# Pads that move the weight pool and the general slots to multiples of 2048 bytes

## The chip, the cores and the metric

One core of one Trainium2 chip runs the whole program. The metric is the device time in microseconds from launch to end; the kernel before is timed at 1852.68 us, the median of 3 runs (1852.58 to 1853.74).

## What is computed

Two layers of a bidirectional encoder on 512 tokens of width 1024, all in fp32. Each layer is half a feed-forward block, a mixer, and half a feed-forward block again:

```
for layer in range(2):
    x = x + 0.5 * swiglu(rms_norm(x), w_gate, w_up, w_down)      # width 2816
    x = x + mixer(rms_norm(x))     # layer 0: dilated attention | Fourier; layer 1: latent attention | S5
    x = x + 0.5 * swiglu(rms_norm(x), w_gate, w_up, w_down)
```

## The kernel before

Tokens lie along the free dimension: an activation tile is 128 channels (partitions) by 512 tokens of 4 bytes, 2048 bytes in each partition. A product that must be good to fp32 is made of three matmuls of type fp32r: each operand is split into a high and a low part, and `mm3` (L136 to L145) multiplies high with high, high with low, low with high. Each of the three is cut into two halves of 256 tokens, and each matmul loads its stationary operand anew:

```
cs = (slice(0, n // 2), slice(n // 2, n)) if n == 512 else (slice(0, n),)
for i, (l, r) in enumerate(((0, 0), (0, 1), (1, 0))):
    for j, c in enumerate(cs):
        mm(out[:, c], lhs[l], rhs[r][:, c], ...)
```

In the trace a matmul is two records: LDWEIGHTS (engine PEld, 128 columns of the stationary operand, 512 bytes of each partition) and MATMUL (engine PE, 256 columns of the moving operand, 1024 bytes of each partition). The trace has 14,592 MATMULs of this line, L145, most of them in the four feed-forward blocks.

On-chip memory (bytes within a partition) is cut into pools, one behind the other, in the order in which `Trunk.__init__` makes them: `const` (gains, x, tables, `ident`), `wp` (the weights: three raw buffers, two high `w_hi`, two low `w_lo`, 8192 bytes each), `tiny` (statistics), `sp` (60 general slots of 2048 bytes: split activations `xgh`, `xgl`, `ah`, `al`, and everything else 512 tokens wide). In front of `const` lies a reserved scratch of 16,384 bytes.

The three pairings of stationary and moving operand that matter here:

- Feed-forward gate and up (outputs `pg`, `pu`) and down (`pd<-ah`, `pd<-al`): the stationary operand is 128 columns of a weight buffer, the moving one half of a slot.
- The input projections of the mixers (`pz`, `pkvu`): the stationary operand is a slot, the moving one a weight buffer.
- Some products of the mixers: both operands lie in slots. Such are the first column block of the output projection (`pd<-mgh,owh` and the like, whose weights `owh`, `owl` are kept in slots), the scores of layer 1 (`sc<-kTh,qTh`), `pq` and `pglu`.

Weights are streamed: `Weights.next` (from L75) has the raw buffers loaded by SyncE up to two units ahead, ScalarE copies a unit to `w_hi` (L49), VectorE makes `w_lo` (L50), while TensorE works on the unit before. A scheduler lays down each engine's instruction order when the program is built. A feed-forward block is two halves, each of 11 gate/up units (96 matmuls each) and 8 down units (66 matmuls each). Between units stand a few matmuls of other shapes: the column sums of the norm (`msc`, L381), the transposes of its result (`rows`, L233), and in two blocks of the S5 tables (`s_pg`, `s_pk`).

Of the kernel before, what the change touches and what calls it, by code (L numbers as in the profile page):

```python
# [5 lines left out]
F32 = mybir.dt.float32  # L6
# [10 lines left out]
HF = NF // 2  # L17
HT = S // 2 + 2
EPS = 1e-6


def f32(ap):
# [3 lines left out]
class Weights:  # L26


    def __init__(self, nc, pool):
        self.nc, self.pool, self.eng = nc, pool, None  # L30
        self.units, self.raw, self.ready = [], {}, {}
        self.pos = self.loaded = self.cut = 0
# [59 lines left out]
class Trunk:  # L92
    def __init__(self, ctx, tc, t):
        self.tc, self.nc, self.t = tc, tc.nc, t
        nc = self.nc
        self.const = ctx.enter_context(tc.tile_pool(name="const", bufs=1))
        self.wp = ctx.enter_context(tc.tile_pool(name="wp", bufs=2))
        self.tiny = ctx.enter_context(tc.tile_pool(name="tiny", bufs=3))
        self.sp = ctx.enter_context(tc.tile_pool(name="sp", bufs=60))
        self.ps = ctx.enter_context(tc.tile_pool(name="ps", bufs=8, space=PSUM))  # L100
        self.W = Weights(nc, self.wp)
        self.gains = self.const.tile([128, 6 * KD], F32, name="gains")
        nc.sync.dma_start(self.gains, t["gains"])
        self.ones = self.const.tile([128, 128], F32, name="ones")
        nc.vector.memset(self.ones, 1.0)
        self.x = [self.const.tile([128, S], F32, name=f"x{c}", tag=f"x{c}") for c in range(KD)]
        self.ident = self.const.tile([128, 128], F32, name="ident")

    def start(self, norm):

        nc = self.nc
        load = lambda c: nc.sync.dma_start(self.x[c], self.t["xT"][c])
        w = self.W.first(KD // 2)
        load(0)
        next(w)
        for c in range(2, KD, 2):
            load(c - 1)
            load(c)
            next(w)
        load(KD - 1)  # L120

        p = self.bank("warm")
        for i in range(10):
            nc.tensor.matmul(p[:, 0:128], self.ones, self.ones, start=True, stop=True)
        self.prep_start()
        for c in range(KD):
            self.scale_split(c, norm)
            if c % 2 == 0:
                next(w)
        nc.sync.dma_start(self.ident, self.t["ident"])  # L130
# [245 lines left out]
    def ms_cols(self, eng=None):  # L376
# [5 lines left out]
        v = self.small(4)("msv")  # L382
        nc.vector.tensor_scalar(out=v, in0=p, scalar1=1.0 / D, scalar2=EPS, op0=ALU.mult, op1=ALU.add)
        return v, self.rsqrt(v, self.small(4), eng)
# [24 lines left out]
    def even_mixer(self, after):  # L409
# [7 lines left out]
        for which in range(2):  # L417
            pz = [self.bank("pz") for _ in range(4)]
            for u in range(2):
# [6 lines left out]
                if epx is None:  # L426
                    msx, rsx = self.ms_cols(nc.gpsimd)
                    epx = self.small(4)("epx")
                    nc.vector.tensor_scalar(out=epx, in0=msx, scalar1=EPS, scalar2=None, op0=ALU.mult)
            for q, z in enumerate(self.head_norm(pz, epx, self.q_rope if which == 0 else self.k_rope, which == 1)):  # L430
# [260 lines left out]
    def odd_mixer(self, after):  # L691
# [21 lines left out]
        epx = new4("epx")  # L713
        nc.vector.tensor_scalar(out=epx, in0=msx, scalar1=EPS, scalar2=None, op0=ALU.mult)
        for k in range(KD):
# [20 lines left out]
        for j in range(2):  # L736
            down(pql[j], wh, wl, 256, j * 128, 128)
            ql.append(self.split(pql[j], "ql", self.lat_gain[:, j:j + 1]))
            if j == 0:
# [10 lines left out]
                nc.vector.tensor_reduce(out=kss, in_=kps, axis=AX.X, op=ALU.add)  # L750
                nc.vector.tensor_scalar(out=kss, in0=kss, scalar1=1.0 / 96, scalar2=EPS, op0=ALU.mult, op1=ALU.add)
                self.rotate(kp[:, :, 0:32], 16, self.kc_rope[0], self.kc_rope[1])
# [49 lines left out]
        def query_eps():  # L802
            nc.vector.tensor_scalar(out=eaq, in0=self.lat_ms(qlsq, 256, epx), scalar1=EPS, scalar2=None, op0=ALU.mult)

# [932 lines left out]
```

## Time and profile before

| | |
|---|---|
| median of 3 runs | 1852.68 us |
| the profiled execution's own time | 1853.05 us |
| its span, first to last instruction | 1851.3 us |
| TensorE busy | 1830.1 us, 99% |
| VectorE, ScalarE, GpSimd busy | 53%, 34%, 5% |
| granted TensorE clock over the span | 0.997 |
| bytes moved | 185.65 MB |

A MATMUL's record is longer than its share of the time, because matmuls are pipelined and the records overlap. What a matmul costs in a dense stretch is the distance from one start to the next, here called its pitch: the length of the stretch over the count of matmuls in it.

### The profile page before, as it was taken

To read this page: it belongs to the slowest core of one execution; us is meant where nothing else is said; L and a number is where in the kernel's file an instruction comes from. 1 tells how busy PE (TensorE), PEld (TensorE's weight loads), DVE (VectorE), ACT (ScalarE), POOL (GpSimd) and SP (SyncE) were. 2 spreads that over 40 slices of the span, in tenths; PEclk is the share of its full clock that TensorE was granted. 3 is DMA by queue.
4 is the path that set the end of the run, shared out by engine and by line. 5 is a ranking of instruction groups with operands and counts; after the bars stand their busy time and mean duration, and the time that the engine had idled before them with its cause. 6 is when DMAs were issued, how large, how long until landed. Compare 5 with 4: busy or idle time off the path is not lost.

```text
span 1851.3 us, 35303 instructions
## 1 busy us (share of the span) xinstructions
PE 1830.1 (99%) x15608; PEld 1810.8 (98%) x15608; DVE 986.0 (53%) x1732; ACT 622.6 (34%) x818; POOL 85.4 (5%) x138
## 2 busy tenths in 40 slices
PE   9999999999999999999999999999989999999999
PEld 9999999999799999999999999999988899999999
DVE  5643444456955954556744434444688654434442
ACT  4321222324953222222332222223366632212321
POOL 0000000011120000000000000000045100000000
PEclk9999999999999999999999999999999999999999
DMA  6223221331122325342322233223144222133221
GB/s 209 93 73 121 95 105 64 117 108 68 37 92 92 113 100 150 112 111 100 128 103 92 79 116 110 89 73 109 69 129 141 79 96 103 64 118 113 85 89 67
DMA packets 63447, 185.65 MB, mean 100 GB/s; under 512 B 27424, under 2 KB 28352, under 8 KB 51136
## 3 DMA queue, kind: packets, MB, share of 16 engines
q1 hardware_dynamic: 63296, 183.41, 29.3%
q8 instruction: 122, 2.00, 0.4%
q14 instruction: 29, 0.24, 0.0%
HBM read 170.79 MB, written 10.49 MB: 98 GB/s over the span
## 4 chain that ended last, share of the span: by engine, by line
PE 95%; DVE 2%; ACT 1%; DMA 1%; issue 0%; POOL 0%; SPq 0%; ACTq 0%; POOLq 0%; DVEq 0%
PE pd L145 30%; PE pu L145 27%; PE pg L145 26%; PE pz L145 4%; PE etp L1447 1%; PE sc L145 1%; PE pf L145 1%; PE pql L145 1%; PE s_py L1230 1%; PE pq L145 1%; PE po L1467 0%; PE po L1468 0%; DVE et_lo L1459 0%; PE sc L533 0%; ACT e L1440 0%
## 5 line engine op out<-in xcount | busy, mean ns | idle before, releaser
L49 ACT ACTIVATE w_hi<-w_raw 128x2048 fp32r<-128x2048 f32 (+4 forms) x175 | 288.6, 1649 | 878.3 <-PE pu L145 449.7
L50 DVE TENSOR_TENSOR w_lo<-w_raw,w_hi 128x2048 fp32r<-128x2048 f32 (+4 forms) x172 | 338.2, 1966 | 166.2 <-ACT w_hi L49 166.0
L145 PE MATMUL pu<-xgh,w_hi 128*128 128x256 f32 x1440 | 282.9, 278 | 0.0
L145 PE MATMUL pu<-xgh,w_lo 128*128 128x256 f32 x1440 | 282.8, 278 | 0.0
L145 PE MATMUL pu<-xgl,w_hi 128*128 128x256 f32 x1440 | 282.6, 278 | 0.0
L145 PE MATMUL pg<-xgh,w_hi 128*128 128x256 f32 x1408 | 277.9, 279 | 1.2 <-ACT w_hi L49 1.2
L145 PE MATMUL pd<-al,w_hi 128*128 128x256 f32 x1408 | 277.5, 277 | 0.0
L145 PE MATMUL pd<-ah,w_lo 128*128 128x256 f32 x1408 | 277.4, 277 | 0.0
L145 PE MATMUL pd<-ah,w_hi 128*128 128x256 f32 x1408 | 276.7, 277 | 0.0
L145 PE MATMUL pg<-xgh,w_lo 128*128 128x256 f32 x1408 | 276.5, 278 | 0.0
L145 PE MATMUL pg<-xgl,w_hi 128*128 128x256 f32 x1408 | 276.4, 278 | 0.0
L145 PEld LDWEIGHTS pu<-xgh,w_hi 128*128 128x128 f32 x1440 | 218.7, 189 | 0.0
L145 PEld LDWEIGHTS pu<-xgh,w_lo 128*128 128x128 f32 x1440 | 218.2, 188 | 0.2 <-DVE w_lo L50 0.2
L145 PEld LDWEIGHTS pu<-xgl,w_hi 128*128 128x128 f32 x1440 | 218.2, 188 | 0.0
L145 PEld LDWEIGHTS pg<-xgh,w_hi 128*128 128x128 f32 x1408 | 213.8, 189 | 1.5 <-ACT w_hi L49 1.5
L145 PEld LDWEIGHTS pd<-ah,w_lo 128*128 128x128 f32 x1408 | 213.9, 188 | 0.0
L145 PEld LDWEIGHTS pd<-ah,w_hi 128*128 128x128 f32 x1408 | 213.6, 188 | 0.0
L145 PEld LDWEIGHTS pg<-xgl,w_hi 128*128 128x128 f32 x1408 | 213.4, 188 | 0.0
L145 PEld LDWEIGHTS pg<-xgh,w_lo 128*128 128x128 f32 x1408 | 213.4, 188 | 0.0
L145 PEld LDWEIGHTS pd<-al,w_hi 128*128 128x128 f32 x1408 | 213.4, 188 | 0.0
L255 DVE TENSOR_TENSOR gn<-pg,rows 128x512 f32<-128x512 f32 x88 | 60.7, 689 | 279.3 <-PE pg L145 279.3
L298 DVE SCALAR_TENSOR_TENSOR x<-pd,x 128x512 f32<-128x512 f32 (+1 forms) x65 | 44.4, 684 | 232.5 <-PE pd L145 232.5
(365 smaller groups left out, 2088.6 us busy)
## 6 DMA issues: line engine op xcount, KB each, us to landing
w_raw<-wa SPq DMA_DIRECT2D x86, 1024.0 KB, 4.9
w_raw<-wb SPq DMA_DIRECT2D x64, 704.0 KB, 4.0
w_raw<-we_qkv SPq DMA_DIRECT2D x6, 1024.0 KB, 4.9
w_raw<-we_out SPq DMA_DIRECT2D x3, 768.0 KB, 4.2
w_raw<-wo_out SPq DMA_DIRECT2D x3, 768.0 KB, 4.1
x<-xT SPq DMA_DIRECT2D x8, 256.0 KB, 5.5
dr_h<-s_h SPq DMA_DIRECT2D x8, 256.0 KB, 2.8
dr_g<-s_g SPq DMA_DIRECT2D x8, 256.0 KB, 3.0
```

The costliest lines, as they stand in the source:

```text
L49: self.nc.scalar.activation(hi, raw, AF.Copy)
L50: (self.eng or self.nc.vector).tensor_tensor(out=lo, in0=raw, in1=f32(hi), op=ALU.subtract)
L145: mm(out[:, c], lhs[l], rhs[r][:, c], start=first and i == 0 and j == 0, stop=last and i == 2, skip_group_check=len(cs) > 1)
L255: nc.vector.tensor_tensor(out=gn, in0=pg, in1=rstd, op=ALU.mult)
L298: nc.vector.scalar_tensor_tensor(out=x, in0=p, scalar=0.5, in1=x, op0=ALU.mult, op1=ALU.add)
L1230: nc.tensor.matmul(py[half][:, k, :], m[i][:, i4, :], r[:, k, :], start=i == 0, stop=i == 2)
L1447: nc.tensor.transpose(p[:, kc, :], e[:, kc * 128:kc * 128 + 128], T.ident)
```

## The change

Two tiles that nothing reads are added, one at the end of what `const` holds when `__init__` returns, one at the start of `tiny`; GpSimd writes zeros into each once. The reserved scratch is halved, which gives the room.

```diff
+PAD_CONST, PAD_TINY = 448, 464
...
         self.ident = self.const.tile([128, 128], F32, name="ident")
+
+        for pool, n in ((self.const, PAD_CONST), (self.tiny, PAD_TINY)):
+            nc.gpsimd.memset(pool.tile([128, n], F32, name="pad", bufs=1), 0.0)
...
-    nc = _bacc.Bacc("TRN2", target_bir_lowering=False, num_devices=1)
+    nc = _bacc.Bacc("TRN2", target_bir_lowering=False, num_devices=1, dynamic_dma_scratch_size=8192)
```

Where the built programs put things, in bytes within a partition:

| | before | rest by 2048 | after | rest by 2048 |
|---|---|---|---|---|
| first raw weight buffer | 39168 | 256 | 32768 | 0 |
| first `w_hi`, first `w_lo` | 63744, 80128 | 256 | 57344, 73728 | 0 |
| first slot (all others follow in steps of 2048) | 104896 | 448 | 100352 | 0 |
| `x0` | 17216 | 832 | 9024 | 832 |
| `ident` | 33600 | 832 | 25408 | 832 |

A stationary operand of a feed-forward matmul starts at a multiple of 512 bytes from its buffer's start, a moving one at 0 or 1024 bytes from its slot's. So the two starts differ by 192 bytes, taken by multiples of 512, in every feed-forward matmul before, and by 0 after. Where both operands lie in slots they differ by 0 before and after.

The order of instructions and what each waits for is the same on all engines, line numbers apart, but for GpSimd. Its program begins so before:

```order
L1730 MEMSET const-float32-0.0 128x1
L1730 MEMSET const-float32-1.0 128x1
L1730 MEMSET const-bfloat16-1.0 128x1
L1730 MEMSET const-uint8-127 128x1
L1721 UNCONDITIONAL_BRANCH
L207 ISA
L207 TENSOR_SCALAR rs_i<-msv 128x4
```

and so after:

```order
L1734 MEMSET const-uint8-127 128x1
L1725 UNCONDITIONAL_BRANCH
L111 MEMSET pad 128x448
L111 MEMSET pad 128x464
L211 ISA
L211 TENSOR_SCALAR rs_i<-msv 128x4
```

Two memsets stand between the start and the engine's first work, the reciprocal root of layer 0's mixer norm (`rs_i<-msv`); nothing else moved.

## Rows read from the trace of the kernel before

**Rows 1.** The page: engines' busy time, and the chain by engine.

```profile
PE 1830.1 (99%) x15608; PEld 1810.8 (98%) x15608; DVE 986.0 (53%) x1732; ACT 622.6 (34%) x818; POOL 85.4 (5%) x138
...
PE 95%; DVE 2%; ACT 1%; DMA 1%; issue 0%; POOL 0%; SPq 0%; ACTq 0%; POOLq 0%; DVEq 0%
```

**Rows 2.** The chain in order of time: start us, length us, engine, output, line, matmuls.

```profile
133.25 59.84 PE pd L145 x528
...
372.61 10.88 PE pz L145 x96
...
526.51 26.87 PE pd L145 x228
...
872.74 62.19 PE pd L145 x528
```

**Rows 3.** Timeline of PE, both operands in slots: start us, us, instruction.

```profile
517.82 0.40 PE L145 MATMUL pd<-mgl,owh 128*128 128x256 f32 x2
518.05 0.40 PE L145 MATMUL pd<-mgh,owl 128*128 128x256 f32 x2
...
519.74 0.64 PE L145 MATMUL pd<-mgh,owh 128*128 128x256 f32 x4
```

**Rows 4.** Timeline of PE round the `rows` transposes at 576.7 us.

```profile
576.26 0.40 PE L145 MATMUL pu<-xgl,w_hi 128*128 128x256 f32 x2
576.50 0.40 PE L145 MATMUL pu<-xgh,w_lo 128*128 128x256 f32 x2
576.73 0.60 PE L233 MATMUL rows<-ident,rs_y 128*128 128x128 f32 x4
...
578.57 0.39 PE L145 MATMUL pg<-xgh,w_hi 128*128 128x256 f32 x2
578.80 0.39 PE L145 MATMUL pg<-xgl,w_hi 128*128 128x256 f32 x2
```

**Rows 5.** L145 by stretches: length, PE busy (MATMULs), clock, DMA share, GB/s.

```profile
111.50:383.50 272.00, 271.99 (x2400) 1.00 0.29 101
577.50:643.50 66.00, 65.16 (x575) 1.00 0.31 108
959.00:1302.00 343.00, 342.75 (x3023) 1.00 0.27 94
1510.70:1847.00 336.30, 336.30 (x2969) 1.00 0.26 91
31.50:111.50 80.00, 79.61 (x674) 1.00 0.25 86
384.30:430.00 45.70, 45.05 (x382) 1.00 0.20 70
526.50:577.50 51.00, 50.16 (x423) 1.00 0.29 104
643.50:959.00 315.50, 308.14 (x2595) 1.00 0.36 115
1458.50:1510.70 52.20, 51.36 (x433) 1.00 0.29 102
```

**Rows 6.** Timeline of PE: matmuls with a moving operand of 64 columns.

```profile
1428.42 0.61 PE L1230 MATMUL s_py<-s_x,s_h 128*128 128x64 f32 x4
1428.87 0.39 PE L1230 MATMUL s_py<-s_U,s_t 128*128 128x64 f32 x2
1429.09 0.61 PE L1230 MATMUL s_py<-s_x,s_h 128*128 128x64 f32 x4
```

**Rows 7.** Timeline of POOL: the last instruction at the start, and the next one.

```profile
0.32 0.10 POOL L1730 MEMSET const-uint8-127<- 128x1 uint8 x1
384.56 0.20 POOL L207 TENSOR_SCALAR rs_i<-msv 128x4 int32<-128x4 int32 x1 [384.14 <-DVE msv L383]
```

**Rows 8.** A group of POOL by line: count, busy us, mean ns, idle us before.

```profile
L1152 POOL TENSOR_TENSOR s_sw<-s_sw,s_sin 128x512 f32<-128x512 f32 x8 | 11.1, 1393 | 5.8 <-DMA s_sw<-s_a 5.5 <-issue 0.3
```

**Rows 9.** Waits: who waited for whom, us in total, times, longest us.

```profile
ACT w_hi L49 <- PE pu L145: 449.7, 80, 10.3
```

## The prediction
> **What bounds the kernel now.** I read the page first [rows 1]: TensorE is busy for 99% of the span and makes up 95% of the chain that ends last. VectorE and ScalarE have nearly half their time free or more, and ScalarE waits for TensorE to free a weight buffer, 449.7 us in all behind `pu` alone [rows 9]. So the time is the number of matmuls times their pitch, and only something that changes the pitch, or stops TensorE, can move it.
>
> The second view is the chain in order of time, which gives the pitch of clean stretches [rows 2]. The down product of the first half of a feed-forward block is 528 matmuls of 256 columns without a break. At 133.25 us it takes 59.84 us, 113.3 ns a matmul. At 872.74 us the same code on the same kind of tiles takes 62.19 us, 117.8 ns. The granted clock is 1.00, 2.4 GHz, in both [rows 5]. 256 columns at that clock are 106.7 ns, so 7 to 11 ns a matmul are lost on something that has two states.
>
> The third view is the timeline at places where the state changes [rows 4]. Before the four `rows` transposes at 576.73 us two matmuls start 0.24 us after the two before them; a microsecond behind the transposes they are 0.23 apart, and stay so. The change comes at an interruption of the row of equal matmuls, and the state then lasts for tens or hundreds of us. Hence a table of L145 by stretches, cut at these changes [rows 5]: the first four stretches are in the quick state, 2400 + 575 + 3023 + 2969 = 8967 matmuls; the last five in the slow one, 674 + 382 + 423 + 2595 + 433 = 4507. (Length over count comes out above the pitch where other matmuls, such as those of the tables, stand in a stretch; the pitch is taken from clean rows, [rows 2, 4].) Of the 14,592 matmuls of L145 some 1118 remain: 194 of the first 31 us and about 924 in the mixers.
>
> The fourth view is what this change turns on. In the output projection at 517 us both operands lie in slots [rows 3]: from the start at 517.82 to the one at 519.74 us there are eight rows of two, 16 matmuls, in 1.92 us, **120.0 ns** each. Same shape, same type, same line, same clock, steady; only the addresses are of another kind. There the stationary and the moving operand start at the same place by multiples of 512 bytes; in the feed-forward blocks they start 192 bytes apart. (With the roles exchanged, `pz`: slot stationary, weights moving, also 192 apart, the pitch is 10.88 us / 96 = 113.3 ns [rows 2].) So the trace has three pitches, 113.3 and 117.8 where the starts differ by 192 and 120.0 where they differ by 0.
>
> **The change, part by part.** *Addresses of weights and slots.* Nothing is removed or reordered; the change gives every pair of weight and slot the difference 0, which today only slot with slot has. The nearest row for the new pairs is therefore [rows 3], and I take its 120.0 ns for all of them. That it is the difference that counts, and not where each operand stands by itself, is a choice: in [rows 3] both operands stand at 448 by 2048 (or a multiple of 512 further), after the change both stand at 0. The trace has no matmul of 256 columns with both at 0. I choose the difference because exchanging the roles of the two operands leaves the pitch alone.
> - Quick state: 8967 x (120.0 - 113.3) ns. With unrounded pitches, 59.84 / 528 = 113.33, that is 8967 x 6.67 = +59.8 us.
> - Slow state: 4507 x (120.0 - 117.78) = +10.0 us.
> - In the mixers about 408 matmuls more pair weights with a slot (924, less those with both in slots and a few of 258 columns): at 2.2 ns +0.9 us. Those with both operands in slots stay at 120.0.
> - Sum +70.7 us.
>
> All of it lies on the path, since in these stretches TensorE waits for nothing. No other engine can come to be the bound: all have the same work and more time for it.
>
> *The bounds of this term.* From above: 120.0 is the longest steady pitch that the trace has at this clock for this shape, so +70.7. From below: with a moving operand of 64 columns, which is far too short to be the limit, a matmul starts every 111.7 ns: six from 1428.42 to 1429.09 us [rows 6]. I read this as what loading 128 columns of a stationary operand costs. If the two reads never met, the pitch would fall to it: 8967 x (111.7 - 113.33) + 4915 x (111.7 - 117.78) = -14.6 - 29.9 = -44.5 us (4915 being 4507 and the 408).
>
> *The two memsets.* They stand behind the start on GpSimd, whose next work begins at 384.56 us after a wait of 384.14 us for VectorE [rows 7]. Each costs between 0.10 us, the memset of one column [rows 7], and 1.39 us, the two-operand product of 512 columns [rows 8]. So at most 2.8 us of 384 idle ones: nothing. Nothing is queued behind them that TensorE needs earlier; without that cover they would cost those 2.8 us once.
>
> *The smaller scratch.* All transfers of the kernel are issued by SyncE, none by GpSimd, and the sizes of transfers stay. ScalarE's copies wait for TensorE [rows 9], so the data are there first. I take zero; a loss would have to appear as ScalarE waiting for DMA.
>
> *A rule against it.* The rows say that addresses matter: 120.0 against 113.3 ns [rows 2, 3]. The Trainium skill, "SBUF — State Buffer", section "Who interferes with whom", gives TensorE two independent read ports, one for the moving operand and one for the weight load, and says that TensorE and ScalarE never wait on anyone; by that the pitch could not depend on where the operands lie, and the sum would be 0 instead of +70.7. The trace does not bear that out. [...]
>
> **The sum against the measured time.** The profiled execution took 1853.05 us, 0.37 above the median; outside its span lie 1.75. 1853.05 + 70.7 = 1923.8 for that execution, 1923.4 against the median.
>
> **The rivals.**
> 1. *Both on a boundary: faster.* What costs may be an operand that does not start on a boundary of the memory: one such operand in the feed-forward pairs (448, with 256 for the other), two in [rows 3]. Then 113.3 and 120.0 are one and two penalties, and after the change there is none. The roles can be exchanged here too, so `pz` does not speak against it. Against it: it has no place for the two states of one pair of addresses. It gives the lower bound, 1852.7 - 44.5 = 1808. It decides from the first feed-forward block on: a pitch under 113 ns there.
> 2. *The change does not do what it is meant to: the addresses do not matter.* Then 120.0 comes from what else goes on in the mixers, and the states come from interruptions alone, which stand where they stood: 1852.7. Against it: 120.0 is as steady as the other two, and the products of weights and slots that follow at 526.51 us in the same output projection go back to 26.87 us / 228 = 117.9 ns [rows 2].
> 3. *Only the states fall otherwise.* The pitches stay, but an interruption leaves the other state behind. All quick: 4915 x -4.45 = -21.9, 1831. All slow: 8967 x 4.45 = +39.9, 1893.
>
> **How the numbers follow.** Forecast 0.55 (its own range 1905 to 1935: a pitch of 118.4 to 121); rival 1 0.20; rival 2 0.14; rival 3 0.11, evenly on both sides. Faster: 0.20 + 0.05 = 0.25. Same, within 0.2%, 3.7 us, which is about what a measurement of this kernel can tell from no change: 0.15. Slower: 0.55 + 0.05 = 0.60. The range leaves out rival 1 and reaches from all quick, 1830, to 1935. The prediction is 1923.
>
> **What would show it.** The clean down stretches of 528 matmuls should take 63.4 us in all eight halves (113.3 ns would be 59.8, rival 1 under 59.5), and the two states should be gone: one pitch, not two. Start distances of 0.24 us everywhere. The slot pairs stay at 120.0. GpSimd's memsets should be over by 3 us. If the eight stretches come out in two kinds again, the difference by 512 is not the cause, and the step "the nearest row is rows 3" is wrong; if ScalarE waits for DMA, the scratch is.

## The result and the profile after

The changed kernel takes **1923.69 us** (median of 4 runs, 1922.40 to 1930.33), the kernel before 1852.82 us (median of 4). The ratio is 1.0389, with a 95% interval of 1.0365 to 1.0413. Between the medians lie 70.9 us; the prediction was +70.7, 1923 us.

The profiled execution of the changed kernel is the longest of the four (1930.33 us, span 1928.5); where its excess lies is told below. TensorE is as busy as before, 99% of the span, and makes up 96% of the chain that ended last, which was 95% in [rows 1]; the page of the kernel after:

```profile
PE 1908.1 (99%) x15608; PEld 1888.9 (98%) x15608; DVE 988.7 (51%) x1732; ACT 622.5 (32%) x818; POOL 86.3 (4%) x140
...
PE 96%; DVE 2%; ACT 1%; issue 0%; POOL 0%; DMA 0%; SPq 0%; DVEq 0%; ACTq 0%
```

The number of matmuls is the same, 15,608, and PE is busy 78.0 us longer. The chain of the kernel after in order of time (start us, length us, engine, output, line, matmuls) answers to [rows 2]; line 145 is line 149 now:

```profile
137.09 63.36 PE pd L149 x528
...
390.53 11.52 PE pz L149 x96
...
546.26 27.34 PE pd L149 x228
...
901.30 63.36 PE pd L149 x528
```

63.36 / 528 = 120.0 ns, in the down products of the first and of the second block alike, which before were 113.3 and 117.8 ns. The trace has seven such unbroken stretches of 528 (matmuls of the S5 tables break the eighth), and all seven take 63.36 or 63.37 us. `pz`, with the slot as the stationary operand, gives 11.52 / 96 = 120.0, and the part of the output projection whose weights come from the weight buffers 27.34 / 228 = 119.9. There is one pitch.

The timeline of PE in the kernel after, first round the `rows` transposes where [rows 4] had two pitches, then in the slot with slot products of [rows 3] (start us, us, instruction):

```profile
597.13 0.40 PE L149 MATMUL pu<-xgh,w_lo 128*128 128x256 f32 x2
597.37 0.60 PE L237 MATMUL rows<-ident,rs_y 128*128 128x128 f32 x4
...
599.23 0.40 PE L149 MATMUL pg<-xgh,w_hi 128*128 128x256 f32 x2
599.47 0.40 PE L149 MATMUL pg<-xgl,w_hi 128*128 128x256 f32 x2
```

```profile
537.33 0.40 PE L149 MATMUL pd<-mgh,owh 128*128 128x256 f32 x2
...
539.25 0.40 PE L149 MATMUL pd<-mgh,owl 128*128 128x256 f32 x2
```

The last two matmuls ahead of the transposes start 0.24 us before these, and behind them the distance is 0.24 us too: the change of pitch at this place is gone. From 537.33 to 539.25 us there are 16 matmuls in 1.92 us, 120.0 ns, as in [rows 3].

The windows view shows where the time went, stage by stage. The cuts are the first matmul of each feed-forward block and of each mixer. Columns: stretch, its length, PE busy (MATMULs), granted clock, DMA share, GB/s. First the kernel before, then the kernel after:

```profile
6.88:372.44 365.56, 365.56 (x3184) 1.00 0.31 109
372.44:553.22 180.78, 177.65 (x1370) 1.00 0.22 75
553.22:934.76 381.54, 381.54 (x3278) 1.00 0.35 113
934.76:1296.03 361.27, 361.27 (x3183) 1.00 0.28 95
1296.03:1486.31 190.28, 177.97 (x1402) 0.97 0.35 107
1486.31:1851.30 364.99, 361.43 (x3182) 1.00 0.26 90
```

```profile
6.66:390.37 383.71, 383.71 (x3185) 1.00 0.30 105
390.37:573.44 183.07, 179.91 (x1370) 1.00 0.21 72
573.44:964.49 391.05, 391.05 (x3278) 1.00 0.34 111
964.49:1345.96 381.47, 381.47 (x3182) 1.00 0.26 90
1345.96:1543.41 197.45, 185.69 (x1403) 0.94 0.33 103
1543.41:1928.50 385.09, 381.62 (x3182) 1.00 0.24 86
```

The four feed-forward blocks cost 18.2 + 9.5 + 20.2 + 20.1 = 68.0 us more. The second block, most of which was in the slow pitch before, pays only 9.5. The mixers pay 2.3 and 7.2 us. The 7.2 is mostly not the change: in the odd mixer the granted clock of this execution is 0.94 against 0.97. TensorE waits there for other engines (it is busy for 185.69 of 197.45 us), and for part of the stretch it is granted the 1.2 GHz level (0.50 from 1464.70 to 1471.40 us). In a later kernel with 120.0 ns everywhere (`d256` below) the same stage took 192.65 us at a clock of 0.95, 2.4 more than before, and the span was 1922.2 us. So some 5 us of the profiled 1928.5 come from the odd mixer of this one execution; that its lower clock is the reason is read from the two stretches, no run tests it.

The two memsets, in the timeline of POOL (compare [rows 7]):

```profile
0.71 0.90 POOL L111 MEMSET pad<- 128x448 f32 x2 [0.29 <-POOLq L1734]
```

They are over at 1.6 us, 0.90 us for both, and nobody waits for them.

### The profile page after: what moved, and what is told of

It reads as the page before. It is cut to its first block, busy times and chain, and to the rows that moved or that the text cites. A ratio compares the mean times of both kernels' runs of the same rounds, so it can differ in the third digit from the quotient of the medians.

```text
span 1928.5 us, 35305 instructions
## 1 busy us (share of the span) xinstructions
PE 1908.1 (99%) x15608; PEld 1888.9 (98%) x15608; DVE 988.7 (51%) x1732; ACT 622.5 (32%) x818; POOL 86.3 (4%) x140
## 4 chain that ended last, share of the span: by engine, by line
PE 96%; DVE 2%; ACT 1%; issue 0%; POOL 0%; DMA 0%; SPq 0%; DVEq 0%; ACTq 0%
PE pd L149 30%; PE pu L149 27%; PE pg L149 26%; PE pz L149 4%; PE sc L149 1%; PE etp L1451 1%; PE s_py L1234 1%; PE pql L149 1%; PE pf L149 1%; DVE et_lo L1463 1%; PE po L1471 1%; PE pq L149 1%; PE po L1472 1%; PE sc L537 0%; PE pqs L836 0%
## 5 line engine op out<-in xcount | busy, mean ns | idle before, releaser
L149 PE MATMUL pu<-xgh,w_hi 128*128 128x256 f32 x1440 | 290.6, 283 | 0.0
L149 PE MATMUL pu<-xgl,w_hi 128*128 128x256 f32 x1440 | 290.4, 283 | 0.0
L149 PE MATMUL pu<-xgh,w_lo 128*128 128x256 f32 x1440 | 290.3, 283 | 0.0
L149 PE MATMUL pg<-xgh,w_hi 128*128 128x256 f32 x1408 | 285.4, 284 | 1.0 <-ACT w_hi L50 1.0
L149 PE MATMUL pd<-al,w_hi 128*128 128x256 f32 x1408 | 285.6, 283 | 0.0
L149 PE MATMUL pd<-ah,w_lo 128*128 128x256 f32 x1408 | 285.2, 283 | 0.0
L149 PE MATMUL pd<-ah,w_hi 128*128 128x256 f32 x1408 | 284.7, 283 | 0.0
L149 PE MATMUL pg<-xgl,w_hi 128*128 128x256 f32 x1408 | 284.1, 283 | 0.0
L149 PE MATMUL pg<-xgh,w_lo 128*128 128x256 f32 x1408 | 283.9, 283 | 0.0
L149 PEld LDWEIGHTS pd<-al,w_hi 128*128 128x128 f32 x1408 | 220.4, 192 | 0.0
```

The costliest lines, as they stand in the source:

```text
L149: mm(out[:, c], lhs[l], rhs[r][:, c], start=first and i == 0 and j == 0, stop=last and i == 2, skip_group_check=len(cs) > 1)
```

## The experiments

Places are given as rests by 2048 bytes, as in the table of addresses ahead of the prediction. Below, "difference" is the start of the slots less the start of the weights. All kernels but the last are the changed kernel with other pads; where a pad is 0 its tile is left out. Line 145 is their line 150. For each the clean down stretches of 528 matmuls are read from the chain in order of time.

### One pad alone, either way, and the scratch alone

`e1_const_only`: weights 0, slots 192.

```diff
-PAD_CONST, PAD_TINY = 448, 464
+PAD_CONST, PAD_TINY = 448, 0
```

> The pad at the end of const and the halved scratch stay, the pad in front of the slots is left out: weights start at a rest of 0 by 2048, slots at 192; starts differ by 192 (by 512) as before the change. Theory (the difference of the two starts decides): the two pitches 113.3 and 117.8 ns come back, none of 120.0 in the feed-forward blocks, about 1853 us (1831 if all is quick, 1893 if all is slow). Rival (it is the weights on the 2048 boundary that cost): 120.0 ns stays, about 1923 us. Rival (one operand on a boundary helps): a pitch under 113 ns, under 1831 us.

Measured: 1853.22 us, ratio to the kernel before 0.9999 (0.9985 to 1.0013).

`e2_tiny_only`: weights 256, slots 256.

```diff
-PAD_CONST, PAD_TINY = 448, 464
+PAD_CONST, PAD_TINY = 0, 464
```

> The pad in front of the slots stays, the one at the end of const is left out: weights and slots both start at a rest of 256 by 2048, so neither is on a boundary, but their starts differ by 0. Theory (difference decides): 120.0 ns in every weight-slot pair, 63.4 us for 528 matmuls, 1923 us, as with both pads. Rival (being on the 2048 boundary is what costs): 113.3 or 117.8 ns, 1831 to 1893 us. Rival (the scratch or the memsets cost): cannot be 120.0 without a gap between matmuls.

Measured: 1926.33 us, ratio 1.0399 (1.0378 to 1.0419).

`e3_scratch_only`: weights 256, slots 448, all of it 8192 bytes lower.

```diff
-PAD_CONST, PAD_TINY = 448, 464
+PAD_CONST, PAD_TINY = 0, 0
```

> Only the halved scratch is kept, no pad: all tiles lie 8192 bytes lower than before the change, rests by 2048 as before (weights 256, slots 448). Theory: no difference from the kernel before, 1853 us, the same two pitches of 113.3 and 117.8 ns at the same places (the states are set by interruptions, which stand where they stood). Rival (the scratch is what costs): slower by up to 70 us, with ScalarE waiting for transfers. Rival (the states fall otherwise when anything moves): another division between 113.3 and 117.8 ns, 1831 to 1893 us.

Measured: 1853.83 us, ratio 1.0007 (0.9997 to 1.0017).

The chain in order of time of `e1_const_only`, then that of `e2_tiny_only`:

```profile
309.36 59.84 PE pd L150 x528
369.20 10.88 PE pz L150 x96
...
870.90 62.19 PE pd L150 x528
```

```profile
328.56 63.36 PE pd L150 x528
391.92 11.52 PE pz L150 x96
...
904.22 63.36 PE pd L150 x528
```

With the weights on the boundary and the slots 192 away, both pitches of the kernel before are back, 59.84 and 62.19 us in the same halves of the same blocks. With neither operand on the boundary but both at the same rest, all is at 120.0 ns. So the boundary of 2048 bytes has no effect of its own, with one operand on it or both: it is the difference of the two starts that counts, as the prediction chose. The halved scratch is worth nothing, and e1 and e3 together also say that the whole region may move without moving the two pitches.

### What the difference is taken by: 256 and 448

`d256` and `d448`: weights at 0, slots at 256 and 448.

```diff
-PAD_CONST, PAD_TINY = 448, 464
+PAD_CONST, PAD_TINY = 448, 16     # d256
+PAD_CONST, PAD_TINY = 448, 64     # d448
```

> Weights at a rest of 0 by 2048, slots at 256: starts differ by 256 (by 512). Theory that the difference by 512 decides, largest loss at 0: no 120.0 ns; 256 is the farthest from 0 there is, so the pitch should be at most that of a difference of 192, 111.7 to 113.3 ns and 1808 to 1831 us if the loss falls with distance. Rival (the difference counts by 256 or less): 120.0 ns, 1923 us as at 0. Rival (any difference but 0 is alike): 113.3 and 117.8 ns, about 1853 us.

Measured: 1924.17 us, ratio 1.0391 (1.0369 to 1.0413).

> Starts differ by 448, which by 256 or by 128 is what 192 is. Theory (modulus 256 or smaller): the two states of the kernel before, 113.3 and 117.8 ns, at the same places, 1853 us. Rival (the modulus is 512 and 0 and 256 are two bad places in it): another pitch than at 192, 1808 to 1923 us.

Measured: 1854.45 us, ratio 1.0004 (0.9994 to 1.0014). The chain of `d256`, then that of `d448`:

```profile
1091.09 63.36 PE pd L150 x528
```

```profile
870.81 62.19 PE pd L150 x528
...
1054.91 59.84 PE pd L150 x528
```

Here my expectation failed. I had written that a difference of 256 would be the farthest from 0 and so at least as good as 192. It is as bad as 0, to the nanosecond. A difference of 448 is as 192, with the quick and the slow pitch in the same blocks. What counts is therefore the difference by 256, not by 512 as the prediction has it; two pairs of places, 0 with 256 and 192 with 448, show this.

### The places in between

Weights at 0, slots at 544, 576, 608, 640, 672 and 224. Places closer together than 32 bytes were not run.

```diff
-PAD_CONST, PAD_TINY = 448, 464
+PAD_CONST, PAD_TINY = 448, 88      # d32
+PAD_CONST, PAD_TINY = 448, 96      # d64
+PAD_CONST, PAD_TINY = 448, 104     # d96
+PAD_CONST, PAD_TINY = 448, 112     # d128
+PAD_CONST, PAD_TINY = 448, 120     # d160
+PAD_CONST, PAD_TINY = 448, 8       # d224
```

> Starts differ by 32. Both theories: 32 is half as far from 0 as 64 is. If the loss is all or nothing between lines of 64 bytes, 32 is still on 0: 120.0 ns, 1923 us. If it falls step by step, between 113.3 and 120.0 ns, 1853 to 1923 us. If only an exact 0 (by 128 or 256) costs: 113.3 and 117.8 ns, about 1853 us.

> Starts differ by 64. Theory B (by 128): 192 and 64 are the same, so 113.3 and 117.8 ns in two states, about 1853 us. Theory A (by 256): 64 is a place of its own, the mirror of 192 (64 behind instead of 64 ahead): if only the distance counts, 1853 us with two states; if it counts which operand lies ahead, anything from 111.7 to 120.0 ns, 1808 to 1923 us.

> Starts differ by 96, between 64 (117.8 ns, one state) and 128 (118.7 ns). Theory (a curve): 117.8 to 118.7 ns, 1882 to 1909 us. Rival (multiples of 32 that are not multiples of 64 have values of their own, as 32 with 116.7 ns suggests): 116.7 ns or less, under 1881 us.

> Weights at a rest of 0 by 2048, slots at 128: starts differ by 128. A difference of 256 gave 120.0 ns, as 0 did, so what counts is the difference taken by 256 or by 128. Theory A (by 256): 128 is as far from 0 as it goes, no 120.0 ns; 113.3 or 117.8 ns as at 192, or less, down to 111.7: 1808 to 1893 us. Theory B (by 128): the same as 0, 120.0 ns in all 528-matmul stretches (63.4 us), 1923 us.

> Starts differ by 160, halfway between 128 (118.7 ns) and 192 (113.3 or 117.8 ns). Theory (a curve): between 113.3 and 118.7 ns, 1831 to 1909 us. Rival (best place between the points taken so far): under 113.3 ns, 1808 to 1831 us, a version that beats both kernels.

> Starts differ by 224, by 256: the mirror of 32. Measured so far, clean stretches by the difference taken by 256: 0 and 256 120.0 ns; 32 116.7; 64 117.8; 128 118.7; 192 and 448 113.3 or 117.8. Theory (one curve by 256 that falls from 0 on either side, with 192 lowest because the slots then lie a quarter ahead): 224 lies between 192 and 256, so 113.3 to 120.0 ns, 1831 to 1923 us, with no stretch under 113.3. Rival (the best place lies between 192 and 256): down to 111.7 ns, 1808 us.

Lines of the chains of `d32`, `d64`, `d96`, `d128`, `d160` and `d224`, in this order:

```profile
318.70 61.60 PE pd L150 x528
380.30 11.36 PE pz L150 x96
```

```profile
321.34 62.18 PE pd L150 x528
```

```profile
327.16 63.36 PE pd L150 x528
```

```profile
322.12 62.65 PE pd L150 x528
```

```profile
323.13 62.65 PE pd L150 x528
385.78 11.52 PE pz L150 x96
...
1656.74 63.36 PE pd L150 x528
```

```profile
322.80 62.48 PE pd L150 x528
385.28 11.20 PE pz L150 x96
```

Put together (pitch: length over 528, in the unbroken stretches of the profiled execution):

| difference by 256 | kernels | pitch of the down stretches, ns | median, us | ratio to before |
|---|---|---|---|---|
| 0 | after; `e2_tiny_only`; `d256` | 120.0 | 1923.69; 1926.33; 1924.17 | 1.0389; 1.0399; 1.0391 |
| 32 | `d32` | 116.7 | 1880.77 | 1.0147 (1.0130 to 1.0164) |
| 64 | `d64` | 117.8 | 1881.95 | 1.0164 (1.0139 to 1.0188) |
| 96 | `d96` | 120.0 | 1923.30 | 1.0375 (1.0356 to 1.0394) |
| 128 | `d128` | 118.7 | 1909.58 | 1.0303 (1.0286 to 1.0320) |
| 160 | `d160` | 118.7, and 120.0 in the last block | 1910.64 | 1.0300 (1.0277 to 1.0322) |
| 192 | before; `e1_const_only`; `e3_scratch_only`; `d448` | 113.3 and 117.8 | 1852.82; 1853.22; 1853.83; 1854.45 | 1; 0.9999; 1.0007; 1.0004 |
| 224 | `d224` | 118.3 | 1901.56 | 1.0254 (1.0233 to 1.0275) |

Four things follow. First, of the eight places in steps of 32 bytes only the one that the kernel had by chance gives its time; the next best, 32 and 64, cost 1.5% and 1.6%. Second, there is no smooth curve with a hole at 0: 96 is as slow as 0, and 32 is better than 64, against what I had expected of `d96` and of `d32` and `d64` in part (the readings "by 128" and "only an exact 0 costs" are both out). `d128`, at 1909.58 us, fell between its two readings (at most 1893, or 1923), and `d160`, at 1910.64, just above the 1909 that the curve allowed. Third, the sign counts: 32 and 224 lie equally far from 0 and give 116.7 and 118.3 ns, 96 and 160 give 120.0 and 118.7. `pz` shows the same from the other side, since there the operands have exchanged roles and the difference its sign: at 32 it runs at 11.36 / 96 = 118.3 ns, the feed-forward pitch of 224; at 224 at 11.20 / 96 = 116.7, that of 32; at 160 at 120.0, that of 96. So the pitch goes by the start of the moving operand less that of the stationary one. Fourth, more than one pitch at one difference, by what went before, is not special to 192.

The stretches of 528 do not show all of this, so here are matmuls of a weight buffer and a slot of `d64` outside them (output projection, timeline of PE), and `pz` of `d96`, whose difference with the sign reversed is 160:

```profile
549.08 0.39 PE L150 MATMUL pd<-mgl,w_hi 128*128 128x256 f32 x2
...
549.76 0.39 PE L150 MATMUL pd<-mgl,w_hi 128*128 128x256 f32 x2
```

```profile
390.52 11.27 PE pz L150 x96
```

Six matmuls from 549.08 to 549.76 us are 113.3 ns: at 64 there are the same two pitches as at 192. `pz` of the kernel before, whose difference with the sign reversed is 64, began at 113.3 ns as well [rows 2]. So 64 is not a place of one pitch, as the expectation of `d96` has it, and the 117.8 ns of the table are not all of it: the profiled execution of `d64` took 1890.03 us and the other three 1880.07 to 1882.40 at the same granted clock, 0.995. That these ran more of their matmuls in the quick pitch is likely but not shown, since only one execution has a trace. At 160 there are three pitches, 11.27 / 96 = 117.4 ns beside 118.7 and 120.0. Shorter stretches of a second pitch stand in `d32` (117.8 ns from 717.98 to 720.10 us) and `d128` (120.0 ns from 687.94 to 690.34 us); at 0, 96 and 224 only one was found.

### Can the slow pitch at 192 be turned into the quick one?

At 192 the kernel still loses time in the slow pitch, 62.19 against 59.84 us for 528 matmuls. In [rows 4] four transposes changed slow into quick. `kick` is the kernel before, memory untouched, with four such transposes put into the second block:

```diff
-    def ffn(self, after, side=iter(()), lag=0, ends=False):
+    def ffn(self, after, side=iter(()), lag=0, ends=False, kick=None):
...
                 next(side, None)
+                if (h, f) == kick:
+                    p = self.bank("kick")
+                    for q in range(4):
+                        nc.tensor.transpose(p[:, q * 128:q * 128 + 128], self.ones[:, 0:1].to_broadcast([128, 128]), self.ident)
...
-    T.ffn(prep(3), s5)
+    T.ffn(prep(3), s5, kick=(1, 3))
```

> The kernel before, with nothing moved in memory (starts differ by 192): four transposes like the `rows` ones, whose result nothing reads, are put among the gate/up matmuls of the second feed-forward block, some 11 us behind the last group of the S5 tables, at about 793 us. From there to the column sums at 946 us stand 1296 matmuls, all at 117.8 ns before. Theory (with starts that differ by 192 the pitch has two states, and an interruption sets which): transposes leave the quick state behind as those at 576.73, 958.27 and 1509.82 us did, so 1296 x 4.45 ns = -5.8 us, less some 0.5 us for the interruption itself: 5.3 us under the kernel before, 0.997 of it, and the down product of 528 behind it takes 59.8 instead of 62.2 us. Rival (what leaves a state behind is not the kind of interruption, as with the transposes at 42.59 us, which left the slow one): the down product stays at 62.2 us, and the time is 0.5 us above the kernel before. Rival (the state belongs to this place in the program): the same, 62.2 us.

Measured: 1855.07 us, ratio 1.0009 (0.9992 to 1.0025): no gain. The timeline of PE round them, and the down product behind them in the chain:

```profile
791.84 0.60 PE L291 MATMUL kick<-ident,ones 128*128 128x128 f32 x4
...
792.99 0.40 PE L145 MATMUL pu<-xgh,w_hi 128*128 128x256 f32 x2
...
793.69 0.40 PE L145 MATMUL pg<-xgh,w_hi 128*128 128x256 f32 x2
```

```profile
871.59 62.19 PE pd L145 x528
```

From 792.99 to 793.69 us six matmuls take 0.70 us, 117 ns; the slow pitch goes on, and the down product stays at 62.19 us. The first rival holds: the kind of interruption does not decide. `kick` alone cannot tell it from the second rival, that the pitch belongs to the place in the program. The first `rows` transposes of the program can. Timeline of PE behind them, in the kernel before and in `e1_const_only`, whose order of instructions is the same:

```profile
42.59 0.60 PE L233 MATMUL rows<-ident,rs_y 128*128 128x128 f32 x4
...
43.26 0.40 PE L145 MATMUL pg<-xgl,w_hi 128*128 128x256 f32 x2
...
43.97 0.40 PE L145 MATMUL pg<-xgl,w_hi 128*128 128x256 f32 x2
```

```profile
41.70 0.60 PE L238 MATMUL rows<-ident,rs_y 128*128 128x128 f32 x4
...
42.63 0.39 PE L150 MATMUL pg<-xgh,w_lo 128*128 128x256 f32 x2
...
43.31 0.39 PE L150 MATMUL pg<-xgh,w_lo 128*128 128x256 f32 x2
```

Six matmuls from 43.26 to 43.97 us in the first, 0.71 us, and six from 42.63 to 43.31 in the second, 0.68 us: behind the same transposes, at the same place in the program, stands the slow pitch in one and the quick in the other, and ahead of them both kernels were in the slow one. So the place does not decide either. What decides stays open.

## Why the prediction was right, point by point

- *TensorE bounds the kernel, and only its pitch can move it.* Right: the same 15,608 matmuls, 78.0 us more of PE's busy time, 77.2 us more of span in the profiled executions, some 5 us of which belong to the odd mixer of this execution.
- *The step that carried the forecast: all weight and slot pairs take the 120.0 ns of [rows 3].* Right: one pitch of 120.0 ns where there were two. That it is the difference of the starts that decides, not the boundary, is shown by `e2_tiny_only` against `e1_const_only`.
- *By multiples of 512.* Wrong in a detail that this sum did not need: `d256` shows 256. The trace of before had only the differences 0 and 192 (in `pz` with the sign reversed), and could not tell 512 from 256.
- *"Exchanging the roles of the two operands leaves the pitch alone."* This was my reason for the difference, and as a rule it is wrong: exchanging the roles changes the sign, and the sign counts (`pz` in `d32` and `d224`). The `pz` of the kernel before had the difference 64, not 192, and 64 happens to have the pitches of 192, 113.3 and 117.8 ns. The choice was right by luck as far as this reason goes; the experiment with both operands at 256 is the reason that holds.
- *The sum.* +70.7 forecast, 70.9 between the medians. That they agree to 0.2 us is luck: the four executions of the changed kernel lie 8 us apart. Stage by stage the terms hold. The third block (934.76 to 1296.03 us before) is the cleanest test of the first term: quick from 959 us on, some 2970 matmuls at 6.67 ns, and slow ahead of that, some 200 at 2.22 ns, are 20.3; measured 20.2. The second block, with 575 matmuls at 113.3 ns and some 2590 at 117.8, tests the second: 3.83 + 5.74 = 9.6; measured 9.5. The first block shows what the sum left out without a reason: some 2300 matmuls quick and 674 slow are 16.8, measured 18.2. The difference is the 194 matmuls of the first 31 us, which the prediction counted and then gave no cost; before, they were in the quick pitch (six from 14.07 to 14.75 us, 113.3 ns), which makes +1.3. The mixers were forecast at some 3.8 in all, since the stretches of [rows 5] reach into them; measured 2.3 and, in `d256`, 2.4, part of which may be the lower clock there (0.95 against 0.97).
- *The range.* "A pitch of 118.4 to 121" for 1905 to 1935 is a slip: by the prediction's own counts 118.4 ns gives 1901 us, and 1905 is 118.7. Nothing else rests on it.
- *The memsets cost nothing.* Right; 0.90 us for both, at the start, inside the bounds of 0.10 and 1.39 us each.
- *The scratch costs nothing.* Right, by `e3_scratch_only`: 1.0007.
- *Rival 1, the boundary makes it faster.* Out: both operands are on it, and the pitch is 120.0; with the weights alone on it (`e1_const_only`) both pitches are as before.
- *Rival 2, addresses do not matter,* and with it the row of the Trainium skill, "SBUF — State Buffer", section "Who interferes with whom", that calls TensorE's two read ports independent. The runs do not bear out what it would mean here: the same TensorE instructions in the same order take 1853.22 us (`e1_const_only`) or 1926.33 us (`e2_tiny_only`) by where their operands lie, and the measurement decides. That the two reads meet at the memory is the reading that fits, but it is only argued: no run shows the reads themselves.
- *Rival 3, only the division between the two pitches changes.* Out for the change, since the two pitches are gone. At an unchanged difference the division does shift when memory moves (behind 41.70 us `e1_const_only` is quick where the kernel before is slow), but `kick`, `e1_const_only` and `e3_scratch_only` all stay within 0.1% of the kernel before.

## What to carry to other kernels

Where matmuls follow each other closely and each loads its weights anew, look at the distance from start to start, not at the record's length, and compare it between pairs of operands that lie differently: 113.3 against 120.0 ns was in the trace before the change, and told its result. "Aligned" is no goal in itself: here equal rests by 256 bytes were the worst place of eight, shared with one other, and the kernel before had the best. The seven other places in steps of 32 bytes cost this kernel 1.5% to 4%, so an edit that only adds a small tile ahead of a pool is worth a look at the pitch behind it.

## What the runs showed of the hardware that was not expected

- In this kernel the pitch of 256-column fp32r matmuls, each with its own weight load, at 2.4 GHz depends on the start of the moving operand less that of the stationary one, by 256 bytes. At 0, 32, ... 224 the long stretches ran at 120.0, 116.7, 117.8, 120.0, 118.7, 118.7 or 120.0, 113.3 or 117.8, and 118.3 ns; at 64 there were stretches at 113.3 ns too, at 160 some at 117.4.
- At a difference of 192, and likewise of 64 and 160, more than one pitch exists, and in the stretches read here one of them lasts until something interrupts the row of matmuls. Behind four transposes stood the quick one at 576.73 us [rows 4] and at 41.70 us in `e1_const_only`, the slow one at 42.59 us and in `kick`. What sets it was not found, and with it stays open whether the slow stretches at 192 can be had quick: by [rows 2, 5] 4507 matmuls at 117.8 instead of 113.3 ns are worth some 20 us.
